# Second feed-forward products: six of sixteen block rows of weights by Strassen's scheme instead of five, in another order

## The chip, the cores and the metric

The kernel runs on one core of one Trainium2 chip. The metric is device time in microseconds (us). Before the change the median of three runs is 1329.37 us (1328.36 to 1329.39).

Names of engines: TensorE does matmuls (PE in the profile; PEld is its load of the stationary operand), VectorE is DVE, ScalarE is ACT, GpSimd is POOL, SyncE is SP, whose queue issues most transfers.

## The reference

A trunk of four layers over 256 tokens and 1024 channels, in float32. Layers 0 and 3 mix tokens by retention, layer 1 by a convolution module, layer 2 by stick-breaking attention. After each mixer comes the feed-forward part that this change is in:

```python
def squared_relu_mlp(xn, w1, w2):
    h = jax.nn.relu(xn @ w1)
    return (h * h) @ w2

# every layer
x = x + m                                                       # m: the mixer
x = x + squared_relu_mlp(rms_norm(x, norm_ffn[i]), ffn_w1[i], ffn_w2[i])
```

`w1` is 1024 x 4096 and `w2` 4096 x 1024. After the last layer comes one more RMS norm with a gain.

## The kernel before

**Products in three matmuls.** Every float32 operand of a large product is split into a high part (a cast to fp32r on ScalarE) and a low part (operand minus high part, on VectorE). A product is then three matmuls: high by high, high by low, low by high. So weights cost TensorE three matmuls per block, ScalarE one cast and VectorE one subtraction.

**Weights.** They come in units of 128 x 1024 numbers, two units to a chunk of 1 MB, by SP's queue into a ring of three `raw` tiles (L348). `PLAN` lists the units in the order of their use. `unit` takes the next: a 1024-wide cast into a tile `wh` (L362) and a 1024-wide subtraction into a tile `wl` (L369). `wh` and `wl` are rings of five tiles each, so a cast waits until TensorE has read the tile five units back.

**The feed-forward part.** `ffn` has two stages. The *up* stage makes, in 16 steps ("up pairs" p = 0 to 15), 256 columns of hidden activations each: matmuls (L573, L577) on the normed input in tiles `z0` to `z7`, sums of two halves (L601 on ScalarE, L602 on VectorE), relu and square (L635, L637; in the last layer the relu is on VectorE, L631), and the split into parts (L412, L413). The *down* stage (`down`) multiplies them by `w2`: 16 block rows kb = 0 to 15 of 256 rows, two units each. The result is four accumulators C[t, c], t a half of the tokens and c a half of the channels. All down matmuls are in `triple` (L689) and keep the order in which they are written; each is 128 x 128 by 128 x 512.

**Plain and fast block rows.** A plain block row is two weight units and 2 x 2 x 2 block products, 24 matmuls. For the block rows in `FAST`, `fast_unit` uses Strassen's scheme (in Winograd's form): seven block products, 21 matmuls, for four sums of weight blocks (T1 to T4, L385) and four sums of activation blocks. The activation sums are made at the end of the up pair of the same number (L644 to L646), and split by L652 and L653. The weight blocks B11 and B21 come as one unit (L362, L369); B22 and T1 to T4 are split by 512-wide casts (L392) and subtractions (L393). Four of the seven products go to accumulators of their own (`mis`), which run through all fast block rows; after the last of them they are added to C (L728 to L735, and L759, L760 after the first half of the rest).

**Order of the block rows.** `MIXED` names those that run first, with all four accumulators open, fast ones among plain ones. `REST` names the plain ones that end the stage: first all of them for c = 0, then for c = 1; while c = 1 runs, C[0,0] and C[1,0] are already scaled, turned and added to the residual (`hook`).

**Who sets the order.** TensorE's down matmuls are fixed by hand. On VectorE and ScalarE a scheduler with a model of the machine orders the instructions when the program is built; each engine then runs its list in order. `issue_after` keeps what is written in its block behind a given instruction.

In layer 0 the down stage also begins to fetch 18 `strip` tiles for the convolution (256 KB each, two with every chunk). In the last layer the final norm's gain lies in `z6` and `z7` (L834).

Of the kernel before, what the change touches and what calls it, by code (L numbers as in the profile page):

```python
# [8 lines left out]
F32 = mybir.dt.float32  # L9
F32R = mybir.dt.float32r  # L10
# [5 lines left out]
P = 128  # L16
# [39 lines left out]

FAST = (5, 6, 13, 14, 15)
MIXED = (0, 5, 1, 2, 6, 3, 13, 4, 14, 7, 15, 8)  # L60
REST = (9, 10, 11, 12)
OUT_ORDER = [(kb, p) for g in (0, 2) for kb in range(4) for p in (g, g + 1)]


# [178 lines left out]
class Trunk:  # L243
# [122 lines left out]
    def unit_lo(self, u):  # L366
        hi, lo, src, cuts = u
        for s in cuts:
            self.nc.vector.tensor_sub(lo[:, s], src[:, s], hi[:, s])  # L369
        return hi, lo  # L370


    def fast_unit(self, name, l, kb):
        nc = self.nc
        ah, al = self.unit((name, l, "a", kb, 0))
        o = self.un % UPC * 1024
        assert PLAN[self.un] == (name, l, "a", kb, 512) and o
        self.un += 1
        b11, b21, b12, b22 = (self.rawt[:, n * 512 : (n + 1) * 512] for n in range(4))
        t1, t2, t3, t4 = (self.tmp() for _ in range(4))  # L380
        out = [(ah[:, :512], al[:, :512]), (ah[:, 512:], al[:, 512:])]
        h = None
        for n, (dst, x, y) in enumerate(((None, b22, None), (t1, b11, b12), (t3, b12, b22), (t2, t1, b22), (t4, t2, b21))):
            if dst is not None:
                nc.vector.tensor_add(dst, x, y)  # L385
            else:
                dst = x
            if n % 2 == 0:
                h = self.wp.tile([P, 1024], F32R, name=self.nm("wh"), tag="wh")
                g = self.wp.tile([P, 1024], F32R, name=self.nm("wl"), tag="wl")  # L390
            c = slice(n % 2 * 512, (n % 2 + 1) * 512)
            nc.scalar.copy(h[:, c], dst)  # L392
            nc.vector.tensor_sub(g[:, c], dst, h[:, c])  # L393
            out.append((h[:, c], g[:, c]))
        return out


# [225 lines left out]
    def ffn(self, i, nxt):  # L623
        nc = self.nc
        last = nxt is None
        h, rb, fast = [], [], {}

        def act(ps):
            t = self.tmp()
            if last:  # L630
# [5 lines left out]
            s = self.tmp()  # L636
# [4 lines left out]
            if p in FAST:  # L641
                x = self.tmp()
                s3, s1, s2, s4 = (x[:, n * P : (n + 1) * P] for n in range(4))
                nc.vector.tensor_sub(v3(x[:, :S], 2, P), v3(s[:, :S], 2, P), v3(s, 2, S)[:, :, P:])  # L644
                nc.vector.tensor_sub(s2, s[:, :P], s1)
                nc.vector.tensor_sub(s4, s[:, S : S + P], s2)  # L646
                n = 2 * FAST.index(p) - 4
                hi, lo = (
                    self.bigt(F32R) if n < 0 else self.zp.tile([P, 512], F32R, name=self.nm("z"), tag=f"z{n + o}")
                    for o in range(2)  # L650
                )
                nc.scalar.copy(hi, x)  # L652
                nc.vector.tensor_sub(lo, x, hi)  # L653
                fast[p] = hi, lo
# [29 lines left out]
    def down(self, i, h, fast, begin, hook):  # L684
        nc = self.nc
# [48 lines left out]
        nc.vector.tensor_add(uq, u, e5)  # L734
        nc.vector.tensor_add(C[1, 1], C[1, 1], uq)  # L735

        if i == 0:
            self.strip_t = []

# [89 lines left out]
    def final(self, i, h, fast):  # L829
        nc = self.nc  # L830
        self.table("sqrt_and_others")
        gain = [self.zp.tile([P, 512], F32, name=self.nm("gain"), tag=f"z{6 + c}") for c in range(2)]
        for c in range(2):
            nc.sync.dma_start(gain[c], self.fin_d[:, c * 512 : (c + 1) * 512])  # L834
        rows = []
        f = self.cp.tile([P, 24], F32, name="fin", tag="fin")

# [6 lines left out]
                ))  # L844

        def hook(C, at):
            if at:
                return
            for t in range(2):
# [908 lines left out]
```

## Time and profile before

| | |
|---|---|
| median of three runs | 1329.37 us (1328.36 to 1329.39) |
| the profiled execution | 1329.23 us |
| its span, from the first to the last instruction | 1327.5 us |
| TensorE busy | 1316.6 us, 99% |
| VectorE busy | 1063.9 us, 80% |
| ScalarE busy | 860.1 us, 65% |
| granted TensorE clock | 1.00 |
| layer 0's down stage in the trace | 293.6 to about 378.5 us |
| layers 1 and 2, the same stage begins at | 569.9 and 862.4 us |
| layer 3, the same stage begins at | 1235.5 us |

How to read the rows that follow: a group's row names line, engine, operation, what is written and read (buffer numbers left out), shapes and count, then busy time and the mean of one in ns, then the engine's idle time just before them and who ended it. A timeline's row has start, length, and in brackets the idle time before it with the one who ended it. The chain of waits is the work that ended last, followed back from the end. Where neighbouring instructions of an engine overlap, the distance of their starts is what one costs, not its length.

### The profile page before, as it was taken

To read this page: it belongs to the slowest core of one execution; us is meant where nothing else is said; L and a number is where in the kernel's file an instruction comes from. 1 tells how busy PE (TensorE), PEld (TensorE's weight loads), DVE (VectorE), ACT (ScalarE), POOL (GpSimd) and SP (SyncE) were. 2 spreads that over 40 slices of the span, in tenths; PEclk is the share of its full clock that TensorE was granted. 3 is DMA by queue.
4 is the path that set the end of the run, shared out by engine and by line. 5 is a ranking of instruction groups with operands and counts; after the bars stand their busy time and mean duration, and the time that the engine had idled before them with its cause. 6 is when DMAs were issued, how large, how long until landed. Compare 5 with 4: busy or idle time off the path is not lost.

```text
span 1327.5 us, 20237 instructions
## 1 busy us (share of the span) xinstructions
PE 1316.6 (99%) x7703; PEld 1133.6 (85%) x7703; DVE 1063.9 (80%) x1805; ACT 860.1 (65%) x1407; POOL 154.1 (12%) x169
## 2 busy tenths in 40 slices
PE   9999999999999999999999999999999999999998
PEld 8988888888899898888888898888888888888886
DVE  7987877779778688798788588798798776798985
ACT  7555546886566478766668678866675555567663
POOL 3554411000009110000000010000020000100000
PEclk9999999999999999999999999999999999999999
DMA  8666655545765655545453355555454554555552
GB/s 312 211 218 223 227 206 191 190 159 201 277 240 152 202 182 193 188 161 220 158 189 130 127 193 189 190 190 210 169 193 171 189 180 160 206 202 191 177 192 94
DMA packets 46049, 253.95 MB, mean 191 GB/s; under 512 B 5376, under 2 KB 10112, under 8 KB 18560
## 3 DMA queue, kind: packets, MB, share of 16 engines
q1 hardware_dynamic: 43360, 245.32, 52.4%
q0 software_dynamic: 1728, 4.72, 0.9%
q10 hardware_dynamic: 864, 2.62, 0.6%
q8 instruction: 60, 0.98, 0.3%
q14 instruction: 37, 0.30, 0.1%
HBM read 245.99 MB, written 6.65 MB: 190 GB/s over the span
## 4 chain that ended last, share of the span: by engine, by line
PE 96%; DVE 2%; ACT 1%; DMA 0%; issue 0%
PE acc L577 22%; PE acc L689 19%; PE acc L573 11%; PE acc L1107 6%; PE acc L1109 6%; PE acc L1108 6%; PE mis L689 3%; PE acc L557 3%; PE acc L558 3%; PE acc L559 3%; PE mis L577 2%; PE acc L1275 1%; PE mis L573 1%; PE acc L1408 1%; DVE wl L393 1%; DVE t L385 1%
## 5 line engine op out<-in xcount | busy, mean ns | idle before, releaser
L369 DVE TENSOR_TENSOR wl<-raw,wh 128x1024 fp32r<-128x1024 f32 (+1 forms) x420 | 512.5, 1231 | 122.1 <-ACT wh L362 119.1
L362 ACT CAST wh<-raw 128x1024 fp32r<-128x1024 f32 (+1 forms) x420 | 433.2, 1041 | 232.4 <-PE acc L689 68.6
L577 PE MATMUL acc<-z,wh 128*128 128x512 f32 x1152 | 399.4, 393 | 0.0
L573 PE MATMUL acc<-z,wl 128*128 128x256 f32 x1152 | 317.6, 280 | 0.0
L689 PE MATMUL acc<-wh,big 128*128 128x512 f32 x800 | 255.9, 391 | 0.0
L577 PEld LDWEIGHTS acc<-z,wh 128*128 128x128 f32 x1152 | 214.2, 187 | 47.1
L573 PEld LDWEIGHTS acc<-z,wl 128*128 128x128 f32 x1152 | 216.9, 189 | 2.4 <-DVE t L602 0.3
L689 PEld LDWEIGHTS acc<-wh,big 128*128 128x128 f32 x800 | 150.2, 188 | 30.7
L689 PE MATMUL acc<-wl,big 128*128 128x512 f32 x400 | 156.2, 390 | 0.5 <-DVE wl L369 0.5
L1107 PE MATMUL acc<-wh,z 128*128 128x512 f32 x352 | 138.6, 394 | 0.0
L1109 PE MATMUL acc<-wh,z 128*128 128x512 f32 x352 | 137.3, 390 | 0.0
L1108 PE MATMUL acc<-wl,z 128*128 128x512 f32 x352 | 137.2, 390 | 0.0
L601 ACT COPY t<-acc 128x256 f32<-128x256 f32 x154 | 53.1, 371 | 57.3 <-PE acc L577 55.4
L689 PEld LDWEIGHTS acc<-wl,big 128*128 128x128 f32 x400 | 75.1, 188 | 17.6 <-DVE wl L369 1.8
L1107 PEld LDWEIGHTS acc<-wh,z 128*128 128x128 f32 x352 | 66.1, 188 | 15.2 <-issue 2.2
L1109 PEld LDWEIGHTS acc<-wh,z 128*128 128x128 f32 x352 | 66.1, 188 | 14.8 <-issue 0.8
L1108 PEld LDWEIGHTS acc<-wl,z 128*128 128x128 f32 x352 | 66.1, 188 | 13.3
L602 DVE TENSOR_TENSOR t<-acc,t 128x256 f32<-128x256 f32 x154 | 59.7, 419 | 17.9 <-ACT t L601 16.0
L392 ACT CAST wh<-t 128x512 fp32r<-128x512 f32 x80 | 47.1, 619 | 35.2 <-DVE t L385 12.3
L557 PE MATMUL acc<-z,wh 128*128 128x256 f32 x224 | 63.7, 284 | 0.0
L492 POOL TENSOR_TENSOR t<-t,t 128x512 f32<-128x512 f32 x15 | 24.2, 1612 | 339.1 <-ACT t L487 308.7
L558 PE MATMUL acc<-z,wh 128*128 128x256 f32 x224 | 63.4, 283 | 0.0
(300 smaller groups left out, 2098.6 us busy)
## 6 DMA issues: line engine op xcount, KB each, us to landing
raw<-in_w SPq DMA_DIRECT2D x214, 1024.0 KB, 4.9
strip<-st POOLq DMA_DIRECT2D x36, 128.0 KB, 4.0
big<-strip SPq DMA_DIRECT2D x18, 256.0 KB, 5.9
big<-in_gn SPq DMA_DIRECT2D x16, 256.0 KB, 5.3
raw<-in_w SPq DMA_DIRECT2D x7, 512.0 KB, 7.4
raw<-hd SPq DMA_DIRECT2D x8, 263.0 KB, 5.2
raw<-hd SPq DMA_DIRECT2D x8, 131.5 KB, 3.6
wh<-in_w ACTq DMA_DIRECT2D x2, 512.0 KB, 6.3
```

Of the source, the lines that this page charges most:

```text
L362: nc.scalar.copy(hi[:, s], src[:, s])
L369: self.nc.vector.tensor_sub(lo[:, s], src[:, s], hi[:, s])
L557: nc.tensor.matmul(o, wh[:, kk, cs], ah, start=st, stop=False, **kw)
L558: nc.tensor.matmul(o, wh[:, kk, cs], al, start=False, stop=False, **kw)
L573: mm = nc.tensor.matmul(ps[m][:, :S], wl[:, kk, cs], a[:, :S], start=first and kk == 0, stop=False, **kw)
L577: nc.tensor.matmul(ps[m], wh[:, kk, cs], a, start=False, stop=last and kk == 3, **kw)
L601: nc.scalar.copy(o[:, s], ps[m][:, S:])
L602: nc.vector.tensor_add(o[:, s], ps[m][:, :S], o[:, s])
L689: mm = nc.tensor.matmul(o, l, r, start=start and n == 0, stop=stop and n == 2, skip_group_check=True)
L1107: nc.tensor.matmul(ps[t], zh[:, s], wh[:, kk], start=k == 0, stop=False, skip_group_check=True)
L1108: nc.tensor.matmul(ps[t], zh[:, s], wl[:, kk], start=False, stop=False, skip_group_check=True)
L1109: nc.tensor.matmul(ps[t], zl[:, s], wh[:, kk], start=False, stop=k == 7, skip_group_check=True)
```

## The change

One block row more is fast: 12 joins 5, 6, 13, 14 and 15. All four accumulators are open over 13 block rows instead of 12. The order of `MIXED` becomes 0, 1, 5, 2, 6, 3, 12, 4, 13, 7, 14, 8, 15: two plain block rows come before the first fast one, and the last is fast. `REST` has three block rows.

In `fast_unit` T1 is made in place, over B12 in the `raw` tile. It then lies beside B22, and one 1024-wide cast and one 1024-wide subtraction split both. T3, the only other reader of B12, is made first. `issue_after` puts the first low part of a fast block row behind the last low part made before it, and the first two adds behind that.

The activation sums of block row 12 take tiles `z0` and `z1`, and the last fast block row `z6` and `z7`; the gain of the final norm moves to two `big` tiles, fetched after the sums that follow the mixed block rows.

```diff
-FAST = (5, 6, 13, 14, 15)
-MIXED = (0, 5, 1, 2, 6, 3, 13, 4, 14, 7, 15, 8)
-REST = (9, 10, 11, 12)
+FAST = (5, 6, 12, 13, 14, 15)
+MIXED = (0, 1, 5, 2, 6, 3, 12, 4, 13, 7, 14, 8, 15)
+REST = (9, 10, 11)
...
     def unit_lo(self, u):
         hi, lo, src, cuts = u
         for s in cuts:
-            self.nc.vector.tensor_sub(lo[:, s], src[:, s], hi[:, s])
+            self.lo_ins = self.nc.vector.tensor_sub(lo[:, s], src[:, s], hi[:, s]).ins
         return hi, lo
 
     def fast_unit(self, name, l, kb):
         nc = self.nc
-        ah, al = self.unit((name, l, "a", kb, 0))
+        out = []
+
+        def parts(*ts):
+            h, g = (self.wp.tile([P, 1024], F32R, name=self.nm(t), tag=t) for t in ("wh", "wl"))
+            a = 0
+            for t in ts:
+                c = slice(a, a + t.shape[1])
+                nc.scalar.copy(h[:, c], t)
+                self.lo_ins = nc.vector.tensor_sub(g[:, c], t, h[:, c]).ins
+                a = c.stop
+            out.extend((h[:, c : c + 512], g[:, c : c + 512]) for c in range(0, a, 512))
+
+        with self.tc.issue_after(self.lo_ins):
+            hi, lo = self.unit((name, l, "a", kb, 0))
+        out = [(hi[:, c : c + 512], lo[:, c : c + 512]) for c in (0, 512)]
         o = self.un % UPC * 1024
         assert PLAN[self.un] == (name, l, "a", kb, 512) and o
         self.un += 1
-        b11, b21, b12, b22 = (self.rawt[:, n * 512 : (n + 1) * 512] for n in range(4))
-        t1, t2, t3, t4 = (self.tmp() for _ in range(4))
-        out = [(ah[:, :512], al[:, :512]), (ah[:, 512:], al[:, 512:])]
-        h = None
-        for n, (dst, x, y) in enumerate(((None, b22, None), (t1, b11, b12), (t3, b12, b22), (t2, t1, b22), (t4, t2, b21))):
...
+        b11, b21, t1, b22 = (self.rawt[:, i * 512 : (i + 1) * 512] for i in range(4))
+        t2, t3, t4 = (self.tmp() for _ in range(3))
+        with self.tc.issue_after(self.lo_ins):
+            nc.vector.tensor_add(t3, t1, b22)
+        with self.tc.issue_after(self.lo_ins):
+            nc.vector.tensor_add(t1, b11, t1)
+        parts(self.rawt[:, 1024:2048])
+        nc.vector.tensor_add(t2, t1, b22)
+        parts(t3, t2)
+        nc.vector.tensor_add(t4, t2, b21)
+        parts(t4)
+        out[2], out[3] = out[3], out[2]
         return out
...
+        def spare(n):
+            if n < 4:
+                return self.bigt(F32R)
+            return self.zp.tile([P, 512], F32R, name=self.nm("z"), tag=f"z{n - 4}")
...
-        gain = [self.zp.tile([P, 512], F32, name=self.nm("gain"), tag=f"z{6 + c}") for c in range(2)]
...
         def hook(C, at):
+            if at == "gain":
+                for c in range(2):
+                    gain.append(self.bigt())
+                    nc.sync.dma_start(gain[c], self.fin_d[:, c * 512 : (c + 1) * 512])
```

The diff does not show how VectorE's list comes out, so three places of it in layer 0 follow. The line numbers of the changed kernel are some 10 higher: L602, L413, L644 to L646 and L653 are L612, L423, L659 to L661 and L664 there; the weight sums L385 are L396 (T3), L398 (T1), L400 (T2) and L402 (T4); the parts L393 are L383; L369 stays.

VectorE at the end of the up stage, before the change: from up pair 15's parts (`big_3277`) to the first low part of plain block row 1 (`wl_3390`). `raw_3332` is fast block row 5.

```order
L413 TENSOR_TENSOR big_3277<-t_688_3272,big_3277 128x256
L385 TENSOR_TENSOR t_709_3339<-t_708_3338,raw_3332 128x512
L393 TENSOR_TENSOR wl_3343<-t_708_3338,wh_3342 128x512
L646 TENSOR_TENSOR t_691_3280<-t_688_3272,t_691_3280 128x128
L393 TENSOR_TENSOR wl_3351<-t_710_3340,wh_3350 128x512
L385 TENSOR_TENSOR t_711_3341<-t_709_3339,raw_3332 128x512
L393 TENSOR_TENSOR wl_3351<-t_709_3339,wh_3350 128x512
L653 TENSOR_TENSOR z_3285<-t_691_3280,z_3284 128x512
L393 TENSOR_TENSOR wl_3359<-t_711_3341,wh_3358 128x512
L369 TENSOR_TENSOR wl_3390<-raw_3387,wh_3389 128x1024
```

VectorE there in the changed kernel: the two low parts of block row 1 (`raw_3340`), up to the first sum of up pair 15 (`acc_3229`). `z_3092` and `z_3159` are the activation sums of block rows 12 and 13.

```order
L369 TENSOR_TENSOR wl_3343<-raw_3340,wh_3342 128x1024
L664 TENSOR_TENSOR z_3092<-t_649_3087,z_3091 128x512
L664 TENSOR_TENSOR z_3159<-t_664_3154,z_3158 128x512
L659 TENSOR_TENSOR t_679_3221<-t_676_3213 128x256
L660 TENSOR_TENSOR t_679_3221<-t_676_3213,t_679_3221 128x128
L369 TENSOR_TENSOR wl_3359<-raw_3340,wh_3358 128x1024
L661 TENSOR_TENSOR t_679_3221<-t_676_3213,t_679_3221 128x128
L423 TENSOR_TENSOR big_3215<-t_676_3213,big_3215 128x256
L423 TENSOR_TENSOR big_3218<-t_676_3213,big_3218 128x256
L612 TENSOR_TENSOR t_689_3273<-acc_3229,t_689_3273 128x256
```

Block row 1's low parts, which were last in that stretch, now stand ahead of up pair 15's sums.

VectorE at a fast block row in the middle of the stage, before: block row 14 (`raw_3625`) with the plain block row ahead of it (`raw_3591`).

```order
L385 TENSOR_TENSOR t_771_3631<-raw_3625 128x512
L385 TENSOR_TENSOR t_773_3633<-raw_3625 128x512
L385 TENSOR_TENSOR t_772_3632<-t_771_3631,raw_3625 128x512
L385 TENSOR_TENSOR t_774_3634<-t_772_3632,raw_3625 128x512
L369 TENSOR_TENSOR wl_3594<-raw_3591,wh_3593 128x1024
L369 TENSOR_TENSOR wl_3610<-raw_3591,wh_3609 128x1024
L369 TENSOR_TENSOR wl_3628<-raw_3625,wh_3627 128x1024
L393 TENSOR_TENSOR wl_3636<-raw_3625,wh_3635 128x512
L393 TENSOR_TENSOR wl_3636<-t_771_3631,wh_3635 128x512
```

VectorE at a fast block row in the changed kernel (`raw_3624`, block row 13):

```order
L369 TENSOR_TENSOR wl_3627<-raw_3624,wh_3626 128x1024
L396 TENSOR_TENSOR t_772_3631<-raw_3624 128x512
L398 TENSOR_TENSOR raw_3624<-raw_3624 128x512
L400 TENSOR_TENSOR t_771_3630<-raw_3624 128x512
L402 TENSOR_TENSOR t_773_3632<-t_771_3630,raw_3624 128x512
L383 TENSOR_TENSOR wl_3636<-raw_3624,wh_3635 128x1024
L383 TENSOR_TENSOR wl_3641<-t_772_3631,wh_3640 128x512
L383 TENSOR_TENSOR wl_3641<-t_771_3630,wh_3640 128x512
L383 TENSOR_TENSOR wl_3648<-t_773_3632,wh_3647 128x512
```

The four adds moved from ahead of the plain block row to behind the fast one's own first low part, and B22 and T1 have one 1024-wide low part (`wl_3636`).

VectorE after the mixed block rows in the changed kernel: block rows 9, 10 and 11 (`raw_3850`, `raw_3888`, `raw_3932`) and the sums of the four extra accumulators.

```order
L369 TENSOR_TENSOR wl_3895<-raw_3888,wh_3894 128x1024
L740 TENSOR_TENSOR big_3838<-mis_3404,big_3836 128x512
L369 TENSOR_TENSOR wl_3917<-raw_3888,wh_3916 128x1024
L742 TENSOR_TENSOR big_3840<-big_3838,big_3837 128x512
L744 TENSOR_TENSOR big_3839<-big_3838,mis_3403 128x512
L369 TENSOR_TENSOR wl_3939<-raw_3932,wh_3938 128x1024
L743 TENSOR_TENSOR acc_3326<-acc_3326,big_3840 128x512
L745 TENSOR_TENSOR big_3841<-big_3839,big_3837 128x512
L369 TENSOR_TENSOR wl_3979<-raw_3932,wh_3978 128x1024
L746 TENSOR_TENSOR acc_3327<-acc_3327,big_3841 128x512
```

Before, the same sums (L729 to L735) also had three low parts among them; L732, the sum into C[0,1], stood behind all three and now, as L743, stands behind two.

More of the change, by code (lines that the diff above doesn't have):

```diff
@@ L378, in fast_unit @@
         self.un += 1
-        b11, b21, b12, b22 = (self.rawt[:, n * 512 : (n + 1) * 512] for n in range(4))
-        t1, t2, t3, t4 = (self.tmp() for _ in range(4))
-        out = [(ah[:, :512], al[:, :512]), (ah[:, 512:], al[:, 512:])]
-        h = None
-        for n, (dst, x, y) in enumerate(((None, b22, None), (t1, b11, b12), (t3, b12, b22), (t2, t1, b22), (t4, t2, b21))):
[L384 to L394, printed above, removed]
+        b11, b21, t1, b22 = (self.rawt[:, i * 512 : (i + 1) * 512] for i in range(4))
[10 more added lines that the diff above has]
+        out[2], out[3] = out[3], out[2]
         return out
@@ L646, in act @@
                 nc.vector.tensor_sub(s4, s[:, S : S + P], s2)
[L647 to L651, printed above, removed]
+                hi, lo = (spare(2 * FAST.index(p) + o) for o in range(2))
                 nc.scalar.copy(hi, x)
@@ L735, in down @@
         nc.vector.tensor_add(C[1, 1], C[1, 1], uq)
+        hook(C, "gain")
         if i == 0:
@@ L831, in final @@
         self.table("sqrt_and_others")
-        gain = [self.zp.tile([P, 512], F32, name=self.nm("gain"), tag=f"z{6 + c}") for c in range(2)]
-        for c in range(2):
-            nc.sync.dma_start(gain[c], self.fin_d[:, c * 512 : (c + 1) * 512])
+        gain = []
         rows = []
```

## The prediction

> **What bounds the kernel now.** I read the page first, then the chain of waits in order of time, then the timeline of TensorE where the chain leaves it, then who waits for whom on the weight loads.
>
> ```profile
> PE 1316.6 (99%) x7703; PEld 1133.6 (85%) x7703; DVE 1063.9 (80%) x1805; ACT 860.1 (65%) x1407; POOL 154.1 (12%) x169
> PE 96%; DVE 2%; ACT 1%; DMA 0%; issue 0%
> ```
>
> TensorE is 96% of the chain that ended last. Its busy share of 99% alone would not say so, since the ends of matmuls are modelled; so I looked at how far apart they start inside the stage that changes. The chain in order of time (start, length, what) shows it:
>
> ```profile
> 302.66 0.68 DVE wl L393
> 303.34 1.15 DVE wl L369
> 304.53 10.96 PE acc L689 x47
> ...
> 329.77 6.12 PE acc L689 x27
> 335.89 0.68 PE mis L689 x3
> ...
> 579.71 1.15 DVE wl L369
> 580.90 10.95 PE acc L689 x47
> ...
> 872.22 1.15 DVE wl L369
> 873.41 10.96 PE acc L689 x47
> ...
> 1235.50 0.87 PE acc L841 x8
> 1236.38 2.74 PE acc L689 x12
> ```
>
> 27 matmuls of 512 columns run from 329.77 to 335.89 with nothing between: 6.12 / 27 = 0.2267 us each. From 304.53 on the chain of layer 0's down stage stays on TensorE. It leaves TensorE once, before 304.53, for two low parts that VectorE makes; the same stands in layers 1 and 2 (580.90, 873.41). In layer 3 the stage opens on TensorE (1235.50) and has no such place. The four rows of TensorE's timeline around it give the size:
>
> ```profile
> 303.43 0.46 PE L689 MATMUL acc<-wl,big 128*128 128x512 f32 x1
> 303.73 0.63 PE L689 MATMUL acc<-wh,big 128*128 128x512 f32 x2
> 304.53 0.50 PE L689 MATMUL acc<-wl,big 128*128 128x512 f32 x1 [0.17 <-DVE wl L369]
> 304.87 0.62 PE L689 MATMUL acc<-wh,big 128*128 128x512 f32 x2
> ...
> PEld acc L689 <- DVE wl L369: 1.8, 3, 0.6
> ```
>
> From 303.43 to 304.87 are four steps, 1.44 us where 4 x 0.2267 = 0.91 would do: 0.53 us lost. The last row (weight loads of this line, all waits: total, times, longest) has three such waits, one in each of layers 0 to 2.
>
> So an edit here pays by what it takes off TensorE, 0.2267 us a matmul, and by these three stalls, as long as VectorE still delivers.
>
> **The matmuls.** A plain block row is 8 block products of 3 matmuls, a fast one 7: 24 against 21. One block row more per layer is fast, in 4 layers: 12 matmuls fewer, which is also what TensorE's instruction lists differ by. 12 x 0.2267 = 2.72 us, all on the path.
>
> The Trainium skill (TensorE: Matmul & The Clock Gate, "Back-to-back issue gap") gives about 131 ns for a 512-column matmul in a stream of load and matmul pairs, and 216 ns for one by itself. By 131 ns the saving would be an estimated 1.57 us and the whole sum, worked out below, an estimated 1326.1 us. The row above has 226.7 ns in just such a stream and decides.
>
> **What pays for them on VectorE and ScalarE.** VectorE's steps, from rows of this stage:
>
> ```profile
> 296.85 1.20 DVE t L385 x2
> 298.05 0.34 DVE big L413
> 298.39 0.20 DVE t L645
> ...
> 302.15 3.89 ACT L362 CAST wh<-raw 128x1024 fp32r<-128x1024 f32 x4
> ...
> 320.13 1.66 ACT L392 CAST wh<-t 128x512 fp32r<-128x512 f32 x3
> ...
> 304.50:315.50 11.00, 10.97 (x48) 9.10 (x49) 11.00 (x15) 5.50 (x8) 0.00 (x0) 1.00 0.74 259
> 315.50:325.70 10.20, 10.20 (x46) 8.45 (x46) 9.16 (x13) 5.96 (x8) 0.00 (x0) 1.00 0.67 260
> 325.70:335.90 10.20, 10.20 (x46) 8.45 (x46) 8.96 (x13) 5.97 (x8) 0.00 (x0) 1.00 0.61 221
> ```
>
> A 512-wide add or low part is 0.60 us, a 1024-wide low part 1.15 (the chain above), a 256-wide one 0.34, a 128-wide one 0.20; a 1024-wide cast on ScalarE is about 0.97 (3.89 / 4), a 512-wide one 0.55 (1.66 / 3). The last two windows (columns: length, then busy time of PE, PEld, DVE, ACT, POOL) are each one plain and one fast block row: TensorE 45 x 0.2267 = 10.2 us, VectorE busy 9.0 to 9.2. Before, the pair costs VectorE 3 x 1.15 + 9 x 0.60 = 8.85 us; now 4 x 1.15 + 7 x 0.60 = 8.80, since B22 and T1 share one 1024-wide low part. ScalarE goes from 3 x 0.97 + 5 x 0.55 = 5.66 to 4 x 0.97 + 3 x 0.55 = 5.53. A pair stays within TensorE's 10.2 us, with 1.4 us to spare. The sixth fast block row puts 7.25 - 2.3 = 4.95 us more on VectorE in the place of a plain one, and block row 12's activation sums (0.34 + 2 x 0.20 + 0.60) another 1.34. Both lie under TensorE: the stage now holds 6 x 4.76 + 10 x 5.44 = 83.0 us of matmuls, against some 6 x 7.25 + 10 x 2.3 = 66.5 us of weight parts on VectorE. I cost them at nothing; uncovered they would be 4 x 6.3 = 25 us.
>
> **Where a fast block row could come late.** The new order has one weak place. The adds of a fast block row now stand behind its first low part, and the cast of B22 waits for T1. From the end of that first low part to the end of the joint one are 4 adds and 1.15: 3.55 us. TensorE needs it 6 matmuls, 1.36 us, after it starts the block row. VectorE must thus be 2.2 us ahead. Queued behind the waiting cast on ScalarE are the casts of T3, T2 and T4 and those of the next plain block row, and VectorE waits for each of these. In the steady pairs, the ring of 5 `wh`/`wl` tiles decides how far ahead it can be: the first tile of the next fast block row comes free when TensorE has read the second tile of the last one, 12 matmuls (2.72 us) after that block row's start. With 0.97 of cast, 1.15 of low part and 3.55, the joint part is ready some 8.4 to 8.5 us after that start, and is wanted at 10.2 + 1.36 = 11.6: 3 us to spare. T4 follows 1.8 us later, and is wanted 2.7 us later.
>
> **The start of the stage, layers 0 to 2.** Before, block row 0 and then fast block row 5 run: VectorE must make ten pieces of block row 5, amid those of up pair 15, before block row 1's first low part, and it comes late. Now block rows 0, 1 and 5 run, and block row 1's two low parts stand ahead of the sums of pair 15.
>
> ```profile
> 289.20 1.22 DVE L369 TENSOR_TENSOR wl<-raw,wh 128x1024 fp32r<-128x1024 f32 x1 [0.53 <-ACT wh L362]
> 293.45 0.43 DVE L602 TENSOR_TENSOR t<-acc,t 128x256 f32<-128x256 f32 x1 [0.28 <-ACT t L601]
> ...
> 293.56 0.48 PE L689 MATMUL acc<-wh,big 128*128 128x512 f32 x1
> ```
>
> TensorE reaches block row 5 after 48 matmuls, 293.6 + 10.9 = 304.5, and wants the joint part at 305.9. VectorE came to pair 15's sums at 293.45. One more fast block (1.34) and 0.55 of weight parts (block row 1's second low part for that of B22) stand before them, against 0.8 of idle in those two rows: about 1.1 later, 294.6. From there to the joint part are two 1024-wide parts, five 512-wide pieces (four adds and an activation part), four of 256 wide, the 256-wide second sum, and some small ones: 2.3 + 3.0 + 1.7 + 0.7 = 7.7, and up to 0.7 of waiting for ScalarE's two steps on pair 15: 303.0. That is 2.9 us early. Next, block row 2: its first cast waits until block row 1's second tile is read at 304.5, ready at 304.5 + 2.1 = 306.6, wanted at 304.5 + 4.76 = 309.3. So the stall should go and not come back further on: 3 x 0.53 = 1.59 us. In layer 3 there is none to win.
>
> **The end of the mixed block rows.** Before, plain block row 8 and 48 matmuls lie between the last fast block row and the first use of C[0,1] in the second half; now 36 matmuls, 8.2 us.
>
> ```profile
> 350.17 19.72 PE acc L689 x87
> ...
> 351.07 0.68 DVE L729 TENSOR_TENSOR big<-mis,big 128x512 f32<-128x512 f32 x1
> 357.48 0.69 DVE L735 TENSOR_TENSOR acc<-acc,big 128x512 f32<-128x512 f32 x1
> ```
>
> The last product of block row 15 ends 3 matmuls after 350.17, at 350.85; the sums take until 357.48 + 0.69, 7.3 us later, with three low parts among them. The new order has three among them too. C[1,1] is wanted 39 matmuls after block row 15, 8.8 us: 1.5 us early. Nothing is paid.
>
> **DMA.** Each layer loads the same bytes. Two strips of layer 0 move from the down stage into the convolution's first units, and the gain moves from `z` tiles to the end of SP's queue.
>
> ```profile
> big<-strip SPq DMA_DIRECT2D x18, 256.0 KB, 5.9
> gain<-in_fin SPq DMA_DIRECT2D x2, 256.0 KB, 2.8
> 356.30:367.20 10.90, 10.90 (x49) 9.03 (x49) 7.07 (x8) 4.20 (x4) 0.37 (x3) 1.00 1.03 407
> ```
>
> The last row's end is the rate: 407 GB/s where strips and weights come together, while a chunk of 1 MB and two strips every 5.44 us ask for 1.5 MB / 5.44 = about 290. The gain has 8 us for its 2.8. Both at nothing; if the two strips held weights back, 0.5 MB at 407 GB/s is 1.3 us.
>
> **Sum.** The profiled execution took 1329.23 us (span 1327.5, 1.7 around it). 1329.23 - 2.72 - 1.59 = 1324.9; the median of the runs is 0.14 above that execution: 1325.1. I say 1325.0.
>
> **Rivals.**
>
> *The stalls stay, in another place* (VectorE's debt at the start is only put off, to block row 2 or 6). For it: VectorE is busy without a gap for 11 us there (the first of the three windows), and its spare time is 1.4 us a pair. Against: 2.7 us to spare at block row 2. It gives 1329.37 - 2.72 = 1326.65. Chance 0.19.
>
> *The joint cast starves the fast block rows: slower.* If VectorE is ever less than 2.2 us ahead at a fast block row, TensorE waits up to 2.2 us there; the first of each layer is the nearest. 4 x 2.2 = 8.8: 1329.37 - 2.72 - 1.59 + 8.8 = 1333.9; at all 24 block rows, 53 us. It decides once VectorE's debt at the start is 2.9 us more than I count. For it: every step of VectorE waits for one of ScalarE and the other way round. Against: the last two windows above, where the same ping-pong ran without a gap on TensorE. Chance 0.08.
>
> *The strips hold the convolution's weights back*: 1325.1 + 1.3 = 1326.4. For it: 1.03 in the DMA column. Against: the rate asked for. Chance 0.05.
>
> *The change does less than it says* (the sums at the end, 1.5 us early by my count, slip by 1.8 to 2.1 us and take 0.3 to 0.6 us of each layer): 1325.1 + 4 x 0.3 to 0.6 = 1326.3 to 1327.5. Chance 0.06.
>
> **How the numbers follow.** The forecast has 0.62. 0.2% is 2.66 us, about what a measurement can tell from no change, so "faster" ends at 1326.71. The forecast and the strips lie below that; of the stalls that stay, at 1326.65, half; of the last case a third: faster 0.62 + 0.05 + 0.10 + 0.02, which I cut to 0.74 for what I did not see. Same 0.18, slower 0.08. The forecast's own range is 1324.3 to 1325.8; taking in the stalls that stay and part of the last case, and a little below for a start that gains more, 1324.0 to 1327.2.
>
> **What would show it.** Right: in layers 0 to 2 the chain stays on TensorE from the stage's first matmul on; no wait of the weight loads of the products for a low part; steps of 0.2267 in every fast block row; VectorE idle about 1 us in each pair. Wrong: a wait of TensorE for a low part or its high part at the third product of a fast block row, for the sums before C[0,1] or C[1,1], or ScalarE waiting for weights in layer 1's first units. The forecast fails if one such wait of half a microsecond or more stands in each layer.

## The result, and the profile after

| | before | after |
|---|---|---|
| median of the timed runs, side by side (20 each) | 1329.72 us | 1326.77 us |
| ratio, 95% interval | | 0.9975 [0.9968, 0.9982] |
| the same kernel timed a second time, beside before (7 runs, 24 of before) | 1330.17 us | 1325.84 us, 0.9967 [0.9955, 0.9978] |
| the profiled execution | 1329.23 us | 1326.9 us |
| its span | 1327.5 us | 1325.1 us |

The forecast was 1325.0 us, 4.3 us less than before, with a range of 1324.0 to 1327.2. The change makes the kernel faster, by 2.9 us in the first comparison and 4.3 in the second. The time alone does not say why: 1326.77 is also close to what the first rival, the stalls that stay in another place, would give (1326.65). The chain and the stages below tell the two apart.

The page of the changed kernel, engines and shares of the chain that ended last:

```profile
PE 1314.0 (99%) x7691; PEld 1131.8 (85%) x7691; DVE 1091.1 (82%) x1829; ACT 864.4 (65%) x1403; POOL 156.6 (12%) x169
...
PE 97%; ACT 1%; issue 1%; DMA 0%; DVE 0%; POOL 0%; ACTq 0%
```

TensorE has 12 matmuls fewer (7691 against 7703), and VectorE's 2% of the chain are gone. The chain of waits in layer 0's down stage shows where they were (start, length, what):

```profile
293.60 11.03 PE acc L700 x48
304.64 0.68 PE mis L700 x3
305.32 1.36 PE acc L700 x6
...
314.84 0.68 PE mis L700 x3
...
359.72 11.57 PE acc L700 x51
```

From the first matmul on the chain stays on TensorE. The first fast block row follows the two plain ones without a gap (293.60 + 11.03 = 304.63), and the next fast one starts 314.84 - 304.64 = 10.20 us later, 45 x 0.2267. No wait of the products (L700) for VectorE is left among the waits of TensorE and of its weight loads.

A measure that leaves the rest of the program out is the **length of a down stage**: from the start of its first matmul by `triple` to the start of its last. For layer 0 the first row is quoted for before (293.56, with the prediction). Here are the last of before and the first and last of after, from TensorE's timelines:

```profile
379.02 0.40 PE L689 MATMUL acc<-wh,big 128*128 128x512 f32 x1
```

```profile
293.47 0.48 PE L700 MATMUL acc<-wh,big 128*128 128x512 f32 x1
...
377.74 0.39 PE L700 MATMUL acc<-wh,big 128*128 128x512 f32 x1
```

Before: 379.02 - 293.56 = 85.46. After: 377.74 - 293.47 = 84.27 (84.28 unrounded). All kernels of this study (us; the sum of the four stages against before, and beside it the difference of the medians of runs timed side by side):

| kernel | layer 0 | 1 | 2 | 3 | stages, against before | runs, against before |
|---|---|---|---|---|---|---|
| before | 85.46 | 85.49 | 85.48 | 84.42 | | |
| before, a second time | 85.46 | 85.47 | 85.47 | 84.42 | 0.0 | -0.5 |
| after | 84.28 | 84.27 | 84.24 | 83.74 | -4.3 | -2.9 |
| after, a second time | 84.26 | 84.28 | 84.24 | 83.74 | -4.3 | -4.3 |
| order alone, five fast | 84.91 | 84.93 | 84.89 | 84.42 | -1.7 | -2.0 |
| new making in the old order | 85.79 | 85.62 | 85.80 | 84.93 | +1.3 | +1.1 |
| old making in the new order, six fast | 84.28 | 84.28 | 84.24 | 83.74 | -4.3 | -5.4 |
| after, halves added on VectorE | 84.27 | 84.27 | 84.28 | 83.74 | -4.3 | -4.4 |
| after, 2 idle adds a fast row | 90.05 | 87.26 | 89.47 | 84.78 | +10.7 | +10.0 |
| after, 4 idle adds a fast row | 95.46 | 94.51 | 95.58 | 90.10 | +34.8 | +33.0 |
| 2 idle adds, not in the last | 85.70 | 85.75 | 85.69 | 84.78 | +1.1 | +0.1 |
| 2 idle adds, in the last alone | 84.96 | 85.00 | 84.96 | 84.06 | -1.9 | -2.1 |
| 2 idle adds, sums in another order | 89.77 | 86.89 | 86.86 | 83.74 | +6.4 | +8.4 |

The stages give the 4.3 us of the forecast, the same to 0.05 us in both executions that were profiled. The runs scatter around that by a microsecond or two, because other stretches of the program vary from execution to execution; the last section shows which.

### The profile page after: what moved, and what is told of

The parts are those of the page before. It is cut to its first block, busy times and chain, and to the rows that moved or that the text cites. A ratio compares the mean times of both kernels' runs of the same rounds, so it can differ in the third digit from the quotient of the medians.

```text
span 1325.1 us, 20247 instructions
## 1 busy us (share of the span) xinstructions
PE 1314.0 (99%) x7691; PEld 1131.8 (85%) x7691; DVE 1091.1 (82%) x1829; ACT 864.4 (65%) x1403; POOL 156.6 (12%) x169
## 4 chain that ended last, share of the span: by engine, by line
PE 97%; ACT 1%; issue 1%; DMA 0%; DVE 0%; POOL 0%; ACTq 0%
PE acc L587 21%; PE acc L700 20%; PE acc L583 11%; PE acc L1121 6%; PE acc L1123 6%; PE acc L1122 6%; PE mis L700 5%; PE acc L567 3%; PE acc L568 3%; PE acc L569 3%; PE mis L587 2%; PE acc L1289 1%; PE mis L583 1%; PE acc L1422 1%; PE mis L447 1%
## 5 line engine op out<-in xcount | busy, mean ns | idle before, releaser
L369 DVE TENSOR_TENSOR wl<-raw,wh 128x1024 fp32r<-128x1024 f32 (+1 forms) x416 | 512.7, 1238 | 116.8 <-ACT wh L362 110.7
L583 PE MATMUL acc<-z,wl 128*128 128x256 f32 x1152 | 317.7, 280 | 0.0
L700 PE MATMUL acc<-wh,big 128*128 128x512 f32 x752 | 242.3, 391 | 0.0
L700 PEld LDWEIGHTS acc<-wh,big 128*128 128x128 f32 x752 | 141.2, 188 | 29.0
L700 PE MATMUL acc<-wl,big 128*128 128x512 f32 x376 | 146.3, 389 | 0.0
L700 PEld LDWEIGHTS acc<-wl,big 128*128 128x128 f32 x376 | 70.6, 188 | 14.4
L612 DVE TENSOR_TENSOR t<-acc,t 128x256 f32<-128x256 f32 x154 | 59.7, 420 | 16.3 <-ACT t L611 14.4
L382 ACT CAST wh<-raw 128x1024 fp32r<-128x1024 f32 x24 | 25.2, 1052 | 62.6 <-DVE raw L398 58.2
L567 PE MATMUL acc<-z,wh 128*128 128x256 f32 x224 | 63.7, 284 | 0.0
L569 PE MATMUL acc<-z,wl 128*128 128x256 f32 x224 | 63.4, 283 | 0.0
```

The source lines that it names most:

```text
L369: self.lo_ins = self.nc.vector.tensor_sub(lo[:, s], src[:, s], hi[:, s]).ins
L567: nc.tensor.matmul(o, wh[:, kk, cs], ah, start=st, stop=False, **kw)
L569: nc.tensor.matmul(o, wl[:, kk, cs], ah, start=False, stop=en, **kw)
L583: mm = nc.tensor.matmul(ps[m][:, :S], wl[:, kk, cs], a[:, :S], start=first and kk == 0, stop=False, **kw)
L612: nc.vector.tensor_add(o[:, s], ps[m][:, :S], o[:, s])
L700: mm = nc.tensor.matmul(o, l, r, start=start and n == 0, stop=stop and n == 2, skip_group_check=True)
```

## The experiments

**1. The order alone.** Before's kernel, five fast block rows; one plain block row more ahead of the first fast one.

```diff
-MIXED = (0, 5, 1, 2, 6, 3, 13, 4, 14, 7, 15, 8)
+MIXED = (0, 1, 5, 2, 6, 3, 13, 4, 14, 7, 15, 8)
```

> The kernel before, with plain block row 1 moved ahead of fast block row 5 and nothing else. Theory: the three stalls of 0.53 us go and nothing comes back: 1.6 us less than the kernel before, and no wait of a product's weight load for a low part. Rival (the debt of VectorE is only put off): such waits come at block row 2 or 6, and the time is the same as before within 0.5 us.

Measured: 1328.13 us against 1330.17, ratio 0.9989 [0.9979, 0.9998]. The chain of this kernel at the place of the old stall:

```profile
294.06 11.03 PE acc L689 x48
305.09 0.68 PE mis L689 x3
```

The stall is gone, and layers 0 to 2 are 0.55, 0.56 and 0.59 us shorter, layer 3 not at all. That is the stall term by itself: 1.70 us for the 1.59 forecast. The runs agree, but with this interval they would not have shown it alone.

**2. The new way of making the weight sums, in the old order.** The changed kernel's `fast_unit` with the block rows of before.

```diff
-FAST = (5, 6, 12, 13, 14, 15)
-MIXED = (0, 1, 5, 2, 6, 3, 12, 4, 13, 7, 14, 8, 15)
-REST = (9, 10, 11)
+FAST = (5, 6, 13, 14, 15)
+MIXED = (0, 5, 1, 2, 6, 3, 13, 4, 14, 7, 15, 8)
+REST = (9, 10, 11, 12)
```

> The changed kernel with the block rows of before: five fast ones, 5 in second place, four in the rest. The new making of a fast block row stays. Theory (the joint part of B22 and T1 needs VectorE 2.2 us ahead, which it is not where 5 comes second): TensorE waits about 1.0 to 1.3 us in each of layers 0 to 2 at the third product of block row 5, where the kernel before waits 0.53 behind it; so 1.4 to 2.4 us slower than the kernel before. Rival (the joint part costs nothing): the stalls stay at 0.53 and the time is that of the kernel before within 0.5 us.

Measured: 1331.3 us, ratio 1.001 [1.0001, 1.002]. The waits of the products' weight loads for VectorE (total, times, longest):

```profile
PEld acc L700 <- DVE wl L383: 2.3, 3, 0.8
PEld acc L700 <- DVE wl L369: 1.4, 4, 0.6
```

The joint low part (L383) comes late in the first fast block row of layers 0 to 2, as forecast for a start without the second plain block row. The wait is at most 0.8 us, not the 1.0 to 1.3 expected. Behind it the low part of plain block row 1 (L369) is late in all four layers; in layer 3, where nothing was forecast, that makes the stage 0.5 us longer. The runs are 1.1 us slower than before's (0.1 to 2.7), less than the 1.4 to 2.4 expected, and would not have excluded the rival's 0.5; its "the joint part costs nothing" is excluded by the waits. The new making depends on the new order; the old order lets it cost more than the old making did.

**3. The old making in the new order.** The reverse: the changed kernel's block rows, with the `fast_unit` of before (four sums in `tmp` tiles, B22 and T1 split by 512-wide steps, no fixed order on VectorE).

```diff
 FAST = (5, 6, 12, 13, 14, 15)
 MIXED = (0, 1, 5, 2, 6, 3, 12, 4, 13, 7, 14, 8, 15)
     def fast_unit(self, name, l, kb):
...
-        with self.tc.issue_after(self.lo_ins):
-            nc.vector.tensor_add(t1, b11, t1)
-        parts(self.rawt[:, 1024:2048])
...
+        t1, t2, t3, t4 = (self.tmp() for _ in range(4))
...
+        for n, (dst, x, y) in enumerate(((None, b22, None), (t1, b11, b12), (t3, b12, b22), (t2, t1, b22), (t4, t2, b21))):
```

> The changed kernel's block rows (six fast, the new order, three in the rest) with the fast block row made as before: four adds into tiles of their own, B22 and T1 split by 512-wide parts, no fixed order on VectorE. Theory: the gain is the number and the order of block rows; the down stages are 84.3 us in layers 0 to 2 and 83.7 in layer 3, as in the changed kernel, and the time is the same within 0.7 us. Rival (the joint part and the fixed order are needed to cover the sixth): waits for low parts in each layer, at least 0.5 us a layer, 2 us and more in all.

Measured: 1325.32 us against 1330.68, ratio 0.9967 [0.9957, 0.9978]. The four stages are those of the changed kernel to the hundredth. So the sum in place and the joint part bring nothing that can be measured: the whole gain is the number and the order of the block rows. What the new making costs VectorE shows in windows of one pair each (plain and fast block row; length, then busy time of PE, PEld, DVE). First this kernel, then the changed one:

```profile
314.70:324.90 10.20, 10.20 (x47) 8.45 (x46) 9.07 (x13) 5.97 (x8) 0.00 (x0) 1.00 0.57 209
324.90:335.10 10.20, 10.20 (x47) 8.45 (x46) 8.60 (x12) 5.97 (x8) 0.00 (x0) 1.00 0.58 206
```

```profile
314.60:324.80 10.20, 10.20 (x47) 8.45 (x46) 9.30 (x12) 5.77 (x7) 0.00 (x0) 1.00 0.61 207
324.80:335.00 10.20, 10.20 (x47) 8.45 (x46) 9.29 (x12) 5.77 (x7) 0.00 (x0) 1.00 0.58 206
```

8.8 us on the average against 9.3: the new making takes 0.5 us more of VectorE for each pair, not 0.05 less. VectorE's timelines (start, length) show a part of the reason; the changed kernel first, then this one:

```profile
319.82 0.69 DVE L396 TENSOR_TENSOR t<-raw 128x512 f32<-128x512 f32 x1
320.55 0.69 DVE L398 TENSOR_TENSOR raw<-raw 128x512 f32<-128x512 f32 x1
321.27 0.69 DVE L400 TENSOR_TENSOR t<-raw 128x512 f32<-128x512 f32 x1
322.00 0.69 DVE L402 TENSOR_TENSOR t<-t,raw 128x512 f32<-128x512 f32 x1
322.61 1.22 DVE L383 TENSOR_TENSOR wl<-raw,wh 128x1024 fp32r<-128x1024 f32 x1
```

```profile
324.00 1.29 DVE L385 TENSOR_TENSOR t<-raw 128x512 f32<-128x512 f32 x2
325.21 1.41 DVE L385 TENSOR_TENSOR t<-t,raw 128x512 f32<-128x512 f32 x2
326.54 3.70 DVE L369 TENSOR_TENSOR wl<-raw,wh 128x1024 fp32r<-128x1024 f32 x3
```

The four adds of the new making start 0.73, 0.72 and 0.73 us apart, and the low part 0.61 after the last: 2.79 us. T1 overwrites what T3 reads, T2 reads T1, T4 reads T2; the low part does not touch T4. The old making's four take 326.54 - 324.00 = 2.54, for T1 and T3 come first, side by side, and only T4 needs the add just ahead of it. An add that needs its neighbour follows some 0.72 us later, another 0.60.

**4. How much cover VectorE has.** Two and four adds of 512 columns, whose result nobody reads, written at the end of each fast block row: 29 and 58 us of VectorE work by 0.6 us each. (Of the two, the scheduler puts one ahead of the joint low part.) The edit is shown for two.

```diff
         parts(t4)
+        idle = self.tmp()
+        for _ in range(2):
+            self.lo_ins = nc.vector.tensor_add(idle, t3, t3).ins
```

> The changed kernel with two more 512-wide adds on VectorE in each of the 24 fast block rows, whose result nobody reads: 48 x 0.60 = 29 us of VectorE work. Theory (a plain and a fast block row leave VectorE 1.4 us): 10.0 us of work in each pair of 10.2 us, no wait of TensorE, the down stages again 84.3 and 83.7 us, the time that of the changed kernel within 0.7 us. Rival (VectorE is already the bound there, or has no lead): each add shows, up to 29 us.

> The same with four adds in each fast block row, 58 us of VectorE work. Theory: a pair now asks 11.2 us of VectorE and has 10.2, so the lead of some 3 us is eaten up at 1.0 us a pair and TensorE then waits about 1 us a pair: 2 to 5 us in each layer's down stage, 8 to 20 us in all. Rival (VectorE has more to spare than I count): no wait of TensorE, the time of the changed kernel.

Measured: 1340.7 us, ratio 1.0079 [1.0066, 1.0092], and 1363.65 us, ratio 1.0259 [1.0243, 1.0275]. Both expectations fell. With two adds a pair no longer fits on VectorE, but only just; the window of one pair of its work is 10.33 us long:

```profile
317.70:328.03 10.33, 10.33 (x47) 8.58 (x46) 10.23 (x14) 5.90 (x8) 0.00 (x0) 1.00 0.58 204
```

VectorE has no gap left (the missing 0.1 us are the starts of dependent adds), and its lead shrinks by 10.33 - 10.20 = 0.13 us a pair. TensorE does not feel that. The first and the last fast block row of this layer on its timeline:

```profile
305.63 0.39 PE L703 MATMUL mis<-wh,big 128*128 128x512 f32 x1
...
356.63 0.39 PE L703 MATMUL mis<-wh,big 128*128 128x512 f32 x1
```

(356.63 - 305.63) / 5 = 10.20 us, as without the adds. The 15.0 us by which the stages are longer than the changed kernel's (10.7 + 4.3) come from another place. Of the products' waits the longest are for one sum, here with two adds, and below with four, where two more rows matter:

```profile
PE acc L703 <- DVE acc L749: 9.4, 4, 3.3
```

```profile
PE acc L703 <- DVE acc L749: 8.9, 4, 2.5
PE acc L703 <- DVE wl L383: 8.5, 12, 0.8
PE acc L703 <- DVE acc L746: 8.0, 4, 2.3
```

L749 is the sum into C[1,1] after the mixed block rows, once a layer, and L746 that into C[0,1]. VectorE comes to them late. Only with four adds do products wait for the low parts of fast block rows too, twelve times, by 0.4 to 0.8 us; that is the mechanism that the expectation for four adds had, and it makes 8.5 of 39.1 us. With two adds the waits for the sum make 9.4 of the 15.0 us; of the others 3.1 lie in layer 0 and 1.9 in layer 2, where the clock fell with the wait (last section). Layer 0, two adds, VectorE's timeline, and TensorE's row of the wait:

```profile
369.98 0.69 DVE L774 TENSOR_TENSOR acc<-acc,big 128x512 f32<-128x512 f32 x1
370.58 0.69 DVE L775 TENSOR_TENSOR acc<-acc,big 128x512 f32<-128x512 f32 x1
371.18 1.21 DVE L369 TENSOR_TENSOR wl<-raw,wh 128x1024 fp32r<-128x1024 f32 x1
372.31 0.69 DVE L749 TENSOR_TENSOR acc<-acc,big 128x512 f32<-128x512 f32 x1
...
373.06 0.79 PE L703 MATMUL acc<-wh,big 128*128 128x512 f32 x1 [2.67 <-DVE acc L749]
```

Two other sums (L774, L775) and a low part stand ahead of it in the list that the scheduler made for this kernel; in the changed kernel's list the same two sums stand behind it. So the sum is late by the added work and by another list, and these two are not parted here. That left two theories for the 15 us: the late sum alone costs the time (A), or the overfull pairs do (B).

**5. Where the adds stand.** Two adds in the first five fast block rows (shown), and in the last alone (`==` for `!=`).

```diff
+        if kb != FAST[-1]:
+            idle = self.tmp()
+            for _ in range(2):
+                self.lo_ins = nc.vector.tensor_add(idle, t3, t3).ins
```

> The two idle adds stay in the fast block rows 5, 6, 12, 13 and 14 and go from the last, 15 (24 us of VectorE work are left of 29). Theory A (the pairs are covered, what cost 14 to 15 us was that the sum into C[1,1] came 2.7 us late after the mixed block rows): only the debt of the last block row is taken off that sum, 2 x 0.6 to 0.72 = 1.2 to 1.4 us a layer; the wait for it falls to 1.2 to 1.5 us and the time to some 1331 us (1329 to 1333). Rival B (the overload of the pairs makes the waits): five of six pairs are still overloaded, 5/6 of the 14.5 us stay: 1338 us.

> The two idle adds only in the last fast block row, 15 (4.8 us of VectorE work). Theory A: the pairs are those of the changed kernel, but the sum into C[1,1] comes later by the two adds (1.2 to 1.4 us) and, in VectorE's list, by one more low part (1.14) and two other sums (1.2) that now stand ahead of it, less 0.8 us of idle time before: 367.7 + 2.9 = 370.6 against a use at 369.2: 1 to 1.5 us of wait a layer, 1331 us (1329 to 1333), about as much as with the adds in the other five. Rival B: one sixth of the 14.5 us: 1328 us, no wait for the sum.

Measured: 1331.2 us, ratio 1.0005 [0.9993, 1.0017], and 1329.02 us, ratio 0.9989 [0.9976, 1.0002], beside 1331.12 of before. TensorE's waits, of the first kernel and of the second:

```profile
PE acc L704 <- DVE acc L750: 4.1, 4, 1.1
```

```profile
PE acc L704 <- DVE acc L750: 1.2, 3, 0.4
```

In both kernels the sum into C[1,1] (L750) is all that the products wait for. With 24 us of added work in the first five fast block rows no pair costs TensorE a wait, and the sum is late by 0.7 to 1.1 us a layer, a little under A's 1.2 to 1.5; theory A's 1331 us is met, B's 1338 is not. With the adds in the last row alone the sum is late as well, but by 0.4 us and not by the 1 to 1.5 that A expected: the list that was built for it has one of the two other sums ahead of it, not both. B expected no wait there. The time, 1329.0, lies between A's 1331 and B's 1328 and decides nothing. The wait is A's, and the effects do not add: the adds in five rows cost 5.4 us of stages over the changed kernel's, in the last one 2.4, in all six 15.0.

**6. The sums in another order.** Two adds in every fast block row; the sums into C[0,0] and C[1,0] put behind that into C[1,1].

```diff
-        nc.vector.tensor_add(C[1, 1], C[1, 1], uq)
+        last = nc.vector.tensor_add(C[1, 1], C[1, 1], uq).ins
...
-                nc.vector.tensor_add(C[0, 0], C[0, 0], e1)
-                nc.vector.tensor_sub(C[1, 0], C[1, 0], u)
+                with self.tc.issue_after(last):
+                    nc.vector.tensor_add(C[0, 0], C[0, 0], e1)
+                with self.tc.issue_after(last):
+                    nc.vector.tensor_sub(C[1, 0], C[1, 0], u)
```

> The kernel with two idle adds in every fast block row, with the two sums of C[0,0] and C[1,0] put behind that of C[1,1] in VectorE's list; the work is the same. Theory A: the wait for C[1,1] falls by these two, 1.2 us a layer, to some 1.5 us: 1340.7 - 4.8 = 1336 us, lower (down to 1332) if the stretch at half clock behind the wait shrinks too. Rival B: nothing changes, 1340 us.

Measured: 1339.55 us, ratio 1.007 [1.0054, 1.0087]. The wait became shorter, three times where it had been four, and 2.3 us at the longest instead of 3.3:

```profile
PE acc L703 <- DVE acc L749: 7.0, 3, 2.3
```

The waits are 2.4 us shorter in all (9.4 to 7.0), half of A's 4.8. VectorE's timeline of layer 0 shows what took the place of the two sums: VectorE stands still ahead of the low part before the sum, for a cast.

```profile
369.66 1.23 DVE L369 TENSOR_TENSOR wl<-raw,wh 128x1024 fp32r<-128x1024 f32 x1 [0.76 <-ACT wh L362]
370.80 0.69 DVE L749 TENSOR_TENSOR acc<-acc,big 128x512 f32<-128x512 f32 x1
```

So taking the two sums away is worth 0.3 to 1.0 us a layer. The stages are 4.3 us shorter in the profiled execution (347.3 against 351.6); that this is near A's 4.8 is luck, for 1.6 of it is layer 2's clock, which did not fall this time (last section). The median fell by 1.2 us only, to 1339.55: by the runs it is B's 1340 and not A's 1336, though the two intervals overlap. In the profiled execution the convolution took 4.0 us more than in that of experiment 4 (194.6 against 190.6; last section), which hides the gain of the stages there. A's mechanism stands by the waits, its size does not, and the runs do not show it.

**7. Layer 3's norm.** In the changed kernel's first profiled execution TensorE waited 0.7 us for an addition on GpSimd, at the norm of layer 3's retention. Here that addition is on VectorE.

```diff
-            nc.gpsimd.tensor_add(sq, sq, self.sq[:, S:])
+            nc.vector.tensor_add(sq, sq, self.sq[:, S:])
```

> The changed kernel with one add of the retention's norm (the two halves of the sum of squares, 128 x 256, two times in the kernel) on VectorE instead of GpSimd. In the profile of the changed kernel TensorE waits 1 us for that add in layer 3, and GpSimd's add before it takes 4.8 us where it took 0.75 us before. Theory A (that wait belongs to the changed kernel's order): 0.9 us less than the changed kernel, about 1325.9 us where the kernel before has 1329.7. Theory B (it is a chance of that one execution): no difference that can be measured.

> The changed kernel once more. Stage times are deterministic: the down stages again 1.2 us shorter in layers 0 to 2 and 0.7 us in layer 3. Theory A: the 1 us wait for GpSimd in layer 3 and the 0.5 us more of waits for instructions in the convolution are there again, and the ratio to the kernel before is again near 0.9975. Theory B: they differ from execution to execution, and one or both are gone in this profile.

> The kernel before once more, for the parts that the change does not touch. Theory: the stretch up to layer 0's down stage, the one with the convolution (190.9 us in its first profile) and the one with layer 3's retention (288.2 us) differ from execution to execution by 0.5 to 1.5 us in the first two; the wait for GpSimd's add in layer 3 stays under 0.3 us, so that the third stays at 288.2 where the changed kernel had 289.4 and 289.0. Rival: the third also varies by 0.7 us and more, and the changed kernel's wait is chance.

Measured: 1325.79 us, ratio 0.9968 [0.9955, 0.998], with the addition on VectorE, and 1325.84, ratio 0.9967 [0.9955, 0.9978], without. Before a second time gave 1330.2, ratio 0.9995 [0.9983, 1.0007]. With the addition on VectorE nothing is gained that can be measured, as theory B had it. The two profiles of before settle it. GpSimd's first addition after a long idle time, in the first profiled execution of before, in that of the changed kernel, and in the second of before:

```profile
959.70 0.75 POOL L930 TENSOR_TENSOR big<-t 128x256 f32<-128x256 f32 x1 [180.11 <-ACT t L921]
```

```profile
956.81 4.81 POOL L944 TENSOR_TENSOR big<-t 128x256 f32<-128x256 f32 x1 [178.86 <-ACT t L935]
```

```profile
961.60 4.81 POOL L930 TENSOR_TENSOR big<-t 128x256 f32<-128x256 f32 x1 [180.11 <-ACT t L921]
...
PE mis L437 <- POOL t L500: 0.7, 1, 0.7
```

The same instruction of the same kernel takes 0.75 us in one execution and 4.81 in the next, and the wait comes with the long one. Of the thirteen executions profiled three have 4.81, before's second and both of the changed kernel, and TensorE waits 0.7, 0.7 and 0.4 us; five have 0.75 and four 3.68, without a wait; the kernel of this section has 5.16, but there the addition that TensorE waits for is on VectorE. So it is no effect of the change, and the expectation for before a second time fell: its stretch ahead of layer 3's stage took 289.2 us, not 288.2. Of the two waits that the expectation for the changed kernel a second time named, this one was there again (0.4 us), and the convolution was back at 190.5 us. Why the addition's length differs stays open.

## Why the prediction was right

**The matmuls: right.** 12 x 0.2267 = 2.72 us was the term. Layer 3, which had no stall to lose, became 84.42 - 83.74 = 0.68 us shorter, three matmuls of 0.2267. The Trainium skill's 131 ns (TensorE: Matmul & The Clock Gate, "Back-to-back issue gap") would have made an estimated 0.39 of it; no run here shows that figure.

**The three stalls: right.** 1.59 us forecast, 1.70 in experiment 1, and in the changed kernel 1.19 + 1.22 + 1.24 - 3 x 0.68 = 1.61. They did not move to block row 2 or 6, the first rival.

**The start of the stage: right, with more to spare than counted.** The joint part of the first fast block row was forecast for 303.0 and wanted at 305.9. VectorE's timeline of the changed kernel:

```profile
300.63 1.22 DVE L383 TENSOR_TENSOR wl<-raw,wh 128x1024 fp32r<-128x1024 f32 x1
```

It ends at 301.8, 1.2 us earlier. Without the second plain block row it was late by up to 0.8 us (experiment 2).

**VectorE's cover in a pair: right in sign, wrong in size.** The step "a pair costs VectorE 8.80 us, 1.4 to spare" used 0.60 us for each of the four adds. They take 2.79 us for 2.40 because each waits for the one ahead of it, and the other parts came out 0.1 longer together: 9.3 us busy, 0.9 to spare. The windows quoted beside the count, of before, had 9.0 to 9.2 already. That the change leaves VectorE's work in a pair about the same was wrong too: experiment 3 has the old making at 8.8. Another number of that step does not follow from it: a fast block row is put at 7.25 us, where its own steps give 2 x 1.15 + 7 x 0.60 = 6.5; it went into the 66.5 us, which were costed at nothing. Nothing of this reached the time, since 9.3 is still less than 10.2. I then expected two adds more to fit as well, from the same count; experiment 4 showed that they do not.

**The weak place: in part another one.** The prediction called the joint part of the fast block rows the weak place, with 3 us to spare in the steady pairs. It ends at 322.61 + 1.22 = 323.8, 9.0 us after the fast block row before it started at 314.84, where 8.4 to 8.5 was said, so 2.6 are to spare. The runs with idle work showed that something else gives way first: the sum into C[1,1] after the mixed block rows, which the prediction had 1.5 us early. That count was right; VectorE's timeline of the changed kernel:

```profile
367.02 0.70 DVE L746 TENSOR_TENSOR acc<-acc,big 128x512 f32<-128x512 f32 x1
```

It ends at 367.7. The last block row's products end three matmuls after 359.72 in the chain above, at 360.4, and C[1,1] is wanted 39 matmuls later, at 360.4 + 8.8 = 369.2. The rival "the sums slip" had a chance of 0.06 and 0.3 to 0.6 us a layer as its price. Its mechanism is the one that the kernels with idle work fell to, at up to 3.3 us a layer. The rival "the joint cast starves the fast block rows" appeared only with 58 us of idle work.

**DMA and the strips: right.** ScalarE's casts wait for weights no longer than before, and in the changed kernel none of these waits lies in layer 1's first units. Its waits, over the whole program, of before and of the changed kernel:

```profile
ACT wh L362 <- DMA raw<-in_w: 6.9, 7, 2.6
```

```profile
ACT wh L362 <- DMA raw<-in_w: 6.5, 7, 2.4
```

**The profile's other sign.** "VectorE idle about 1 us in each pair": 10.20 - 9.30 = 0.90.

**The rest of the program** was taken as fixed, and that was the one thing the sum left out. In the first pair of profiles the spans differ by 2.4 us and the stages by 4.3. The other 1.9 are 0.7 in layer 1's convolution and 1.2 ahead of layer 3's down stage, of which TensorE's wait for GpSimd is 0.7. Both vary in executions of before as well (191.6 and 289.2 us the second time, 190.9 and 288.2 the first). What follows a stage did not become longer: from layer 1's to layer 2's it is 207.0 us before and 207.1 after, and from layer 3's to the end 6.9 in both. So the time came out 1.8 us above the forecast with its terms right to 0.05; that it lies inside the range, by 0.4 us, owes something to luck.

## What to carry to other kernels

When one stage is bound by one engine from end to end, count that engine's instructions and its few stalls, and measure the stage by the starts of its first and last instruction: it shows 0.05 us where the whole time scatters by two. Adds that each need the one just ahead of them cost more than the same adds among others (0.72 us against 0.60 here), so merging casts and working in place can take an engine more time while it issues less. And look for the weak place at the end of a phase, where one late sum meets an accumulator that is wanted at a fixed time, rather than in the steady state, where a small debt is carried along.

## What the hardware showed beside it

**A wait of 2.3 us can halve TensorE's clock.** In the kernel of experiment 6 the same wait of 2.33 us for the sum stands in layers 0, 1 and 2. The three stretches behind it, 3 us each (the column after the five engines is the granted clock):

```profile
371.55:374.55 3.00, 3.00 (x9) 2.33 (x9) 1.14 (x2) 1.28 (x2) 0.00 (x0) 0.62 1.06 404
655.96:658.96 3.00, 3.00 (x18) 2.57 (x18) 1.13 (x2) 1.87 (x3) 0.00 (x0) 1.00 0.81 287
949.89:952.89 3.00, 3.00 (x18) 2.57 (x18) 1.14 (x2) 1.28 (x2) 0.00 (x0) 1.00 0.80 276
```

Layer 0 has 9 matmuls starting where the others have 18, at a clock of 0.62; it takes 2.9 us longer than layers 1 and 2, of which 1.1 are another wait, for ScalarE. Cut finer, the clock is 1.00 up to 372.25, 0.7 us after the wait's end, then half for 3.41 us, and 1.00 again:

```profile
372.25:375.66 3.41, 3.41 (x12) 2.62 (x11) 0.44 (x1) 1.56 (x3) 0.00 (x0) 0.50 1.05 410
```

With two adds (experiment 4) a wait of 2.67 us halved the clock in layer 0 and not in layer 1, one of 3.33 halved it in layer 2, and waits of 1.1 us and less (experiment 5) never did. The Trainium skill (TensorE: Matmul & The Clock Gate, Part 1) has the clock fall after an idle window of some 3.4 us, by a window that runs on by itself. The second part agrees with a wait of one length having two outcomes; the first does not agree with 2.33 us being enough.

**TensorE also waits in the convolution, at fixed places of its list.** Among the small matmuls of layer 1 (128x32 by 128x128) it stands still at places 128 matmuls with their loads apart, and nothing that the profile shows releases it ("issue"). In the changed kernel, and in that of experiment 5 without adds in the last row:

```profile
450.30 0.28 PE L1289 MATMUL acc<-raw,big 128*32 128x128 f32 x1 [0.85 <-issue]
```

```profile
453.93 0.37 PE L1293 MATMUL acc<-raw,big 128*32 128x128 f32 x1 [3.03 <-issue]
...
453.90:458.00 4.10, 4.07 (x22) 2.97 (x22) 0.29 (x1) 0.31 (x1) 0.00 (x0) 0.50 0.64 207
```

The same place cost 0.85 us in one execution and 3.03 in another, and behind the long one the clock was 0.50: layer 1's stretch ahead of its down stage took 196.3 us in the latter where it took 189.9 to 192.1 in the profiles without such a wait. In experiment 6's execution the same place cost 2.48 us, the clock fell as well, and the stretch took 194.6. The long wait alone moved an execution by some 4 to 6 us, and no change of the down stage touches that place. That the waits come every 256 instructions, and in before too, suggests that instructions arrive late; no run tested it.
